# Out-projection of a short-convolution block: float32 sums in memory, spread residual loads, early operand work a step later, last tiles by token block

## The chip, the cores and the metric

The kernel runs on 1 core of one Trainium2 chip. The metric is the device time of one launch in microseconds (us). Engines are named as the profile names them: PE is TensorE (matmuls; PEld its weight loads), DVE is VectorE, ACT is ScalarE, POOL is GpSimd and SP is SyncE, which here only issues DMAs. POOL issues DMAs too, on a queue of its own.

## What is computed

With DEPTH = 1 only the first layer and the final norm remain of the reference:

```python
x = x + short_conv_mixer(rmsnorm(x, norm0_w), conv0_w_in, conv0_w_conv, conv0_w_out)
return rmsnorm(x, norm_f_w)

def short_conv_mixer(h, w_in, w_conv, w_out):
    b_gate, c_gate, u, z = jnp.split(h @ w_in, 4, axis=-1)
    cu = c_gate * u
    conv = causal depthwise convolution of cu, width 3
    y = b_gate * conv * jax.nn.silu(z)
    return y @ w_out
```

x has 1024 tokens of 2048 float32 values; w_in is 2048 x 8192, w_out 2048 x 2048.

## The kernel before

**Arithmetic.** Every float32 operand of a matmul is split into a rounded high part and the rest, a low part (`split`, lines 104 to 106: a copy on ACT, then a subtraction on DVE), and three matmuls (high x high, high x low, low x high, `PASSES`) make one product. Two-by-two blocks of each product are formed by seven sums of blocks instead of eight products (`PRODUCTS` 1, 5, 6, 2, 7, 3, 4); the sums of operands that this needs are made on DVE (`sub` line 109, `add` line 112).

**Order of the work.** All work is a list of steps, each with `loads`, `add`, `split`, `mm` and `evac`. The loop at the end emits, at step i, the loads, adds and splits of the steps ahead, then the matmuls of step i and what follows from them. `early` steps (i < 6) load one step ahead and split nothing ahead; later ones load 6 steps ahead, add 3 and split 2 ahead. Each engine takes its instructions strictly in the resulting order, so an instruction that waits holds up all behind it on its engine.

**Stages.** (1) `classical`, 8 steps, 384 matmuls: the first block of 128 channels, all four gates, plain products. Its operands need no token scale, so that x can be squared and summed meanwhile (`square`, in the `evac` of steps 0 to 3); the scale `rbc` comes from the sums through a power on POOL and two small DMAs (`token_scale`, lines 193 to 195). From step 4 on, `evac` also prepares the operands of all later blocks (class `XPrep`: load `xa`, `norm` line 137, then `item(r, j)` for each product). The 8 sums in PSUM are scaled out of it in step 7 (`g<-pc`, line 338). (2) `block`, 30 blocks of 7 steps of 24 matmuls, 5040 in all; the result y of 128 channels goes to `y_dram` (line 223, POOL queue) at the end of each block in the second half. The last block's y is made right after its last matmuls. (3) `out_block(db)`, twice 28 steps (7 products r by 4 pieces u) of 24 matmuls, 1344 in all. A step needs a sum of pieces of w_out (`wo`) and a sum of pieces of y. With db = 0 the y pieces are read from `y_dram` (`yr`, line 478, SP queue, 512 KB in rows of 2 KB), summed on DVE, split to high and low (`Y`, pool `xp`), used, and the split pair is stored to `s_dram` (`sd`, line 539, POOL queue, 1 MB); with db = 1 the pair is read back (line 502, POOL queue, 1 MB) and used as it is.

**Pools.** `xp` has 14 tiles of 8 KB per partition (operands X, then Y and the residual rows `st`), `t4` 16 of 4 KB (all raw loads, sums, gates), `wp` 3 (split weights), PSUM 8 banks.

**Ends.** `open_out` (lines 603 to 614), called one step ahead of the out-projection, loads all eight 1 MB residual tiles `st` and the weight `wf` of the final norm on the POOL queue. `evac` adds each finished sum to its residual; after the last product of a token block, `finish` (lines 616 to 634) forms the norm and stores the tile: sum of squares on ACT, a reduction and a scale on DVE, a power on POOL, a scaling shared by ACT and DVE, two stores. In the very last step (r = 4, u = 3, db = 1) the matmuls run token block by token block (`order`).

```python
for i, s in enumerate(steps):
    early = i < 6
    upto("load", i + (2 if early else LOAD_AHEAD + 1))
    ...
    if i == first_out - 1:
        open_out()
    upto("add", i + 1 if early else i + AHEAD + 2)
    upto("split", i + (1 if early else AHEAD + 1))
    s.mm()
    s.evac()
```

## Time and profile before

| | us |
|---|---|
| median of 3 runs (1603.18 to 1604.12) | 1603.95 |
| the profiled execution's own time | 1604.42 |
| its span in the profile | 1602.6 |
| PE busy (share of the span) | 1551.5 (97%) |
| DVE busy | 1030.0 (64%) |
| ACT busy | 508.6 (32%) |
| POOL busy | 106.2 (7%) |
| moved by DMA | 323.61 MB, mean 202 GB/s |
| chain that ended last: PE | 84% |
| chain that ended last: DMA | 8% |
| chain that ended last: DVE | 5% |

The span is what the profiler saw between the first and the last instruction; the 1.8 us between it and the execution's own time lie around it. Busy shares are means over the whole span, and the three stages have different limits, so the page's share says little about one of them: times are taken from the stretch in which they lie. A busy PE is not one at full speed, since its clock can be lowered (column PEclk, the granted clock: 1.00 is 2.4 GHz, 0.50 is 1.2 GHz).

### The profile page before, as it was taken

To read this page: it belongs to the slowest core of one execution; us is meant where nothing else is said; L and a number is where in the kernel's file an instruction comes from. 1 tells how busy PE (TensorE), PEld (TensorE's weight loads), DVE (VectorE), ACT (ScalarE), POOL (GpSimd) and SP (SyncE) were. 2 spreads that over 40 slices of the span, in tenths; PEclk is the share of its full clock that TensorE was granted. 3 is DMA by queue.
4 is the path that set the end of the run, shared out by engine and by line. 5 is a ranking of instruction groups with operands and counts; after the bars stand their busy time and mean duration, and the time that the engine had idled before them with its cause. 6 is when DMAs were issued, how large, how long until landed. Compare 5 with 4: busy or idle time off the path is not lost.

```text
span 1602.6 us, 17246 instructions
## 1 busy us (share of the span) xinstructions
PE 1551.5 (97%) x6777; PEld 1278.1 (80%) x6777; DVE 1030.0 (64%) x1116; ACT 508.6 (32%) x633; POOL 106.2 (7%) x200
## 2 busy tenths in 40 slices
PE   9899999999999999999999999999999797899996
PEld 7678888888888888888888888888888685788885
DVE  4598555554555544467777777777776785766344
ACT  7364333333333333222222222222222232441234
POOL 0000010100000100200000000000001110110001
PEclk9999999999999999999999999999999898999998
DMA  9715453443444443953344434334336999999755
GB/s 365 292 47 194 141 182 121 167 161 131 145 161 145 174 163 119 409 222 125 128 135 129 137 122 134 129 119 130 121 118 263 343 400 387 392 417 336 269 195 210
DMA packets 83953, 323.61 MB, mean 202 GB/s; under 512 B 8976, under 2 KB 9504, under 8 KB 73888
## 3 DMA queue, kind: packets, MB, share of 16 engines
q1 hardware_dynamic: 55872, 180.38, 33.1%
q0 software_dynamic: 26704, 137.93, 22.5%
q10 hardware_dynamic: 1296, 4.20, 0.7%
q8 instruction: 53, 0.87, 0.2%
q14 instruction: 28, 0.23, 0.0%
HBM read 230.20 MB, written 92.28 MB: 201 GB/s over the span
## 4 chain that ended last, share of the span: by engine, by line
PE 84%; DMA 8%; DVE 5%; issue 1%; ACT 1%; SPq 0%; POOL 0%; DVEq 0%; POOLq 0%; ACTq 0%
PE pa L415 40%; PE pc L415 20%; PE pb L415 10%; PE poa L549 7%; DMA yr<-y_dram 3%; PE poc L549 3%; PE pob L549 3%; DMA xsq<-in_x_dram 2%; DMA wo<-in_w_out_dram 2%; PE pc L301 1%; DVE wo L106 1%; DVE Y L106 1%; DVE yr L109 1%; DVE xa L137 1%; DVE wo L109 0%
## 5 line engine op out<-in xcount | busy, mean ns | idle before, releaser
L415 PE MATMUL pa<-X,w 128*128 128x512 f32 x2880 | 669.2, 390 | 9.4 <-DVE g L112 9.4
L415 PEld LDWEIGHTS pa<-X,w 128*128 128x128 f32 x2880 | 541.6, 188 | 122.2 <-DVE g L112 9.8
L415 PE MATMUL pc<-X,w 128*128 128x512 f32 x1440 | 336.1, 389 | 0.0
L415 PEld LDWEIGHTS pc<-X,w 128*128 128x128 f32 x1440 | 270.4, 188 | 56.0
L106 DVE TENSOR_TENSOR w<-wi,w 128x1024 fp32r<-128x1024 f32 x150 | 183.7, 1224 | 164.4 <-ACT w L105 163.5
L105 ACT CAST w<-wi 128x1024 fp32r<-128x1024 f32 x150 | 157.5, 1050 | 248.9 <-PE pa L415 189.9
L549 PE MATMUL poa<-wo,Y 128*128 128x512 f32 x768 | 178.6, 394 | 4.8 <-DVE wo L106 4.8
L549 PEld LDWEIGHTS poa<-wo,Y 128*128 128x128 f32 x768 | 146.1, 190 | 36.2 <-DVE wo L106 5.6
L415 PE MATMUL pb<-X,w 128*128 128x512 f32 x720 | 168.1, 389 | 0.0
L415 PEld LDWEIGHTS pb<-X,w 128*128 128x128 f32 x720 | 135.2, 188 | 28.0
L112 DVE TENSOR_TENSOR g<-pa,g 128x512 f32<-128x512 f32 x150 | 103.3, 689 | 74.1 <-PE pa L415 72.2
L105 ACT CAST w<-wt 128x1024 fp32r<-128x1024 f32 x60 | 63.4, 1056 | 247.2 <-PE pc L415 126.1
L549 PE MATMUL poc<-wo,Y 128*128 128x512 f32 x384 | 93.0, 403 | 11.6 <-DVE wo L106 9.3
L301 PE MATMUL pc<-xc,wc 128*128 128x512 f32 x384 | 90.6, 397 | 9.6 <-ACT xc L280 8.7
L106 DVE TENSOR_TENSOR wo<-wo,wo 128x1024 fp32r<-128x1024 f32 x56 | 68.4, 1222 | 47.5 <-ACT wo L105 47.4
L549 PEld LDWEIGHTS poc<-wo,Y 128*128 128x128 f32 x384 | 74.8, 196 | 29.1 <-DVE wo L106 10.0
L441 ACT COPY g<-pa 128x512 f32<-128x512 f32 x90 | 52.9, 588 | 139.1 <-PE pa L415 137.4
L301 PEld LDWEIGHTS pc<-xc,wc 128*128 128x128 f32 x384 | 72.7, 191 | 27.5 <-ACT xc L280 9.9
L105 ACT CAST wo<-wo 128x1024 fp32r<-128x1024 f32 x56 | 58.6, 1049 | 111.1 <-PE poa L549 48.2
L106 DVE TENSOR_TENSOR w<-wt,w 128x1024 fp32r<-128x1024 f32 x60 | 73.5, 1225 | 21.7 <-ACT w L105 21.5
L112 DVE TENSOR_TENSOR g<-pc,g 128x512 f32<-128x512 f32 x90 | 61.8, 687 | 37.8 <-PE pc L415 37.8
L109 DVE TENSOR_TENSOR wt<-wi,wi 128x1024 f32<-128x1024 f32 x60 | 73.4, 1223 | 3.0 <-DMA pd<-g 1.6
(83 smaller groups left out, 897.6 us busy)
## 6 DMA issues: line engine op xcount, KB each, us to landing
wi<-in_w_in_dram SPq DMA_DIRECT2D x120, 512.0 KB, 3.8
wo<-in_w_out_dram SPq DMA_DIRECT2D x64, 512.0 KB, 9.9
pd<-g POOLq DMA_DIRECT2D x60, 512.0 KB, 3.3
g<-pd SPq DMA_DIRECT2D x60, 512.0 KB, 4.7
sd<-Y POOLq DMA_DIRECT2D x28, 1024.0 KB, 8.6
Y<-sd POOLq DMA_DIRECT2D x28, 1024.0 KB, 6.6
yr<-y_dram SPq DMA_DIRECT2D x36, 512.0 KB, 10.8
xd<-xo POOLq DMA_DIRECT2D x28, 512.0 KB, 2.9
```

The source lines that it names most:

```text
L105: nc.scalar.copy(h, raw)
L106: nc.vector.tensor_tensor(l, raw, h.bitcast(F32), op=ALU.subtract)
L109: nc.vector.tensor_tensor(o, a, b, op=ALU.subtract)
L112: nc.vector.tensor_tensor(o, a, b, op=ALU.add)
L137: nc.vector.scalar_tensor_tensor(t, t, n0[:, k:k + 1], rbc, op0=ALU.mult, op1=ALU.mult)
L301: nc.tensor.matmul(state["ps"][2 * s + gi][h], wv[:, wz, gi, jj, s, :], xs[:, xz, h * NB:(h + 1) * NB], start=(a == 0 and jj == 0 and wz = ...
L415: nc.tensor.matmul(ps[where, s], wv[:, wz, j, s, :], xt[:, j % 2, xz, :], start=(r in (1, 5, 2) and j == 0 and wz == 0 and xz == 0), stop= ...
L441: nc.scalar.copy(o, ps[where, s])
L549: nc.tensor.matmul(ps[where, tb], Y[r, u][:, yz, jj * NB + tb * P:jj * NB + (tb + 1) * P], w["w"][:, wz, jj * NB:(jj + 1) * NB], start=(r ...
```

## The change

It has four parts.

1. **Stored sums.** For the products 5, 6, 3 and 7 the float32 sum of y pieces (512 KB) is stored to `s_dram` in the `add` of db = 0, and with db = 1 read back on the SP queue and split again. For the products 1, 2 and 4, which use a plain piece of y, nothing is stored, and db = 1 reads `y_dram` once more. So 28 stores and 28 loads of 1 MB become 16 stores of 512 KB on POOL and 28 loads of 512 KB on SP, and db = 1 gets 28 more splits.
2. **Spread residual loads.** The eight `st` tiles are loaded by twos at the steps -1, 0, 3 and 4 of the out-projection (`open_rows`), and `wf` at step 6, in one tile of `xp` instead of two of `t4`.
3. **First block.** Loading and splitting go one step further ahead from step 2 on (loads i + 3, splits i + 2); `norm` and the first items move from the `evac` of step 4 to that of step 5, half of step 5's to step 6; from step 6 on less is loaded, added and split ahead than before, until step 8.
4. **Last tiles.** The matmuls of (r = 4, db = 1) of u = 2 and u = 3 are emitted together, token block by token block, 12 matmuls each.

```diff
-    s_dram = {r: dram.tile([4, P, 2, 1024], F32R, name=f"sd_{r}") for r in PRODUCTS}
+    s_dram = {r: dram.tile([4, P, 1024], F32, name=f"sd_{r}") for r in (5, 6, 3, 7)}
...
                 if a == 4:
                     for j in range(4):
                         first_x.load(j, 0)
-                    for j in range(4):
-                        first_x.norm(j, 0)
-                    for j in range(4):
-                        first_x.item(1, j)
                 if a == 5:
                     for j in range(4):
                         first_x.load(j, 1)
                     for j in range(4):
+                        first_x.norm(j, 0)
+                        first_x.item(1, j)
+                    for j in range(2):
                         first_x.norm(j, 1)
-                    for j in range(4):
                         first_x.item(5, j)
                 if a == 6:
+                    for j in range(2, 4):
+                        first_x.norm(j, 1)
+                        first_x.item(5, j)
                     for r in (6, 2):
...
+                elif r in s_dram:
+                    w["y"] = {"s": f4(f"ys_{r}_{u}")}
+                    nc.sync.dma_start(w["y"]["s"], s_dram[r][u])
                 else:
-                    t = hl(xp, f"Y_{db}_{r}_{u}")
-                    nc.gpsimd.dma_start(t, s_dram[r][u])
-                    Y[r, u] = t
+                    n = {1: (0, 0), 2: (0, 1), 4: (1, 1)}[r]
+                    w["y"] = {n: yraw(n[0], n[1], u, f"{db}{r}{n[0]}{n[1]}")}
...
+                    if r in s_dram:
+                        nc.gpsimd.dma_start(s_dram[r][u], y[0, 0] if r == 7 else schain[u])
...
-                if db == 0:
...
+                if db == 1 and r in s_dram:
+                    src = y["s"]
+                else:
                     src = schain[u] if src is None else y[src]
-                    t = hl(xp, f"Y_{db}_{r}_{u}")
-                    split(src, t[:, 0, :], t[:, 1, :])
-                    nc.gpsimd.dma_start(s_dram[r][u], t)
-                    Y[r, u] = t
+                t = hl(xp, f"Y_{db}_{r}_{u}")
+                split(src, t[:, 0, :], t[:, 1, :])
+                Y[r, u] = t
...
+                if r == 4 and db == 1 and u >= 2:
+                    order = [(u, jj, tb) for tb in range(4) for u in (2, 3) for jj in range(2)] if u == 3 else []
...
+    def open_rows(th, tb):
+        t = xp.tile([P, D], F32, name=f"st_{th}_{tb}", tag="hl")
+        r0 = (th * 4 + tb) * P
+        nc.gpsimd.dma_start(t, x[r0:r0 + P, :])
...
+    def open_wf():
+        t = xp.tile([P, D], F32, name="wf", tag="hl")
...
     for i, s in enumerate(steps):
-        early = i < 6
-        upto("load", i + (2 if early else LOAD_AHEAD + 1))
+        early = i < 2
+        upto("load", i + (2 if early else 3 if i < 8 else LOAD_AHEAD + 1))
...
-        if i == first_out - 1:
-            open_out()
-        upto("add", i + 1 if early else i + AHEAD + 2)
-        upto("split", i + (1 if early else AHEAD + 1))
+        n = i - first_out
+        if n in (-1, 0, 3, 4):
+            for tb in range(2):
+                open_rows(n > 0, tb + 2 * (n in (0, 4)))
+        if n == 6:
+            open_wf()
+        upto("add", i + (1 if early else 2 if i < 8 else AHEAD + 2))
+        upto("split", i + (1 if early else 2 if i < 8 else AHEAD + 1))
```

**First place: VectorE ahead of the second step of the first block.** `w_1_5` is the split weight of that step (product 5), `wt_1` its sum, `X_r` the prepared operands of product r, `s` their sums. Before, `w_1_5` stands right behind X_2 and ahead of the eight `g` rows:

```order
L109 TENSOR_TENSOR s_1_682<-s_1_682,xa_582 128x512
L106 TENSOR_TENSOR X_6_0_777<-s_0_674,X_6_0_777 128x512
L109 TENSOR_TENSOR wi_1_00_697<-wi_1_11_701,wt_1_705 128x1024
L106 TENSOR_TENSOR X_6_1_784<-s_1_682,X_6_1_784 128x512 x2
L106 TENSOR_TENSOR X_2_0_790<-xa_662,X_2_0_790 128x512
L106 TENSOR_TENSOR X_2_0_790<-xa_664,X_2_0_790 128x512
L106 TENSOR_TENSOR X_2_1_795<-xa_666,X_2_1_795 128x512
L106 TENSOR_TENSOR X_2_1_795<-xa_668,X_2_1_795 128x512
L106 TENSOR_TENSOR w_1_5_801<-wt_1_705,w_1_5_801 128x1024
L338 TENSOR_TENSOR g_0_852<-pc_0_207,rbc 128x512
L338 TENSOR_TENSOR g_0_852<-pc_1_208,rbc 128x512
```

After, the same row stands behind the eight `g` rows, all of X_7 and half of X_3:

```order
L106 TENSOR_TENSOR X_7_1_859<-xa_593,X_7_1_859 128x512
L109 TENSOR_TENSOR xa_595<-xa_595 128x512
L109 TENSOR_TENSOR s_0_684<-xa_661,s_0_684 128x512
L109 TENSOR_TENSOR s_0_684<-xa_663,s_0_684 128x512
L106 TENSOR_TENSOR X_7_1_859<-xa_595,X_7_1_859 128x512
L106 TENSOR_TENSOR X_3_0_866<-s_0_684,X_3_0_866 128x512 x2
L109 TENSOR_TENSOR wt_1_876<-wi_1_01_786,wi_1_00_693 128x1024
L109 TENSOR_TENSOR s_1_753<-xa_665,s_1_753 128x512
L109 TENSOR_TENSOR wi_1_00_693<-wi_1_11_872,wt_1_876 128x1024
L106 TENSOR_TENSOR w_1_5_879<-wt_1_876,w_1_5_879 128x1024
L106 TENSOR_TENSOR X_3_1_918<-s_1_753,X_3_1_918 128x512
```

Counted from the first `norm` row to this split, VectorE has 44 rows' worth of work before (8 norms, 6 splits of `xc`, 6 full-width rows, 24 half-width rows) and 60 after (8, 2, 5 and 45): four of the six `xc` splits and one weight split went ahead of the norms, and 21 half-width rows, the eight `g` rows among them, came in.

**Second place: the POOL queue at the start of the out-projection.** `st` are the residual rows, `y_dram<-g` the results of the last two blocks, `sd` the stored operands. Before, all residual rows stand together:

```order
L608 DMA st_0_8111<-in_x_dram 128x2048
L539 DMA sd_164<-Y_1_0_8075 128x2048
L608 DMA st_1_8114<-in_x_dram 128x2048
L223 DMA y_dram<-g_3_7557 128x1024
L608 DMA st_2_8117<-in_x_dram 128x2048
L608 DMA st_3_8120<-in_x_dram 128x2048
L608 DMA st_0_8123<-in_x_dram 128x2048
L608 DMA st_1_8126<-in_x_dram 128x2048
L608 DMA st_2_8129<-in_x_dram 128x2048
L608 DMA st_3_8132<-in_x_dram 128x2048
L613 DMA wf_8135<-in_norm_f_w_dram 128x1024
L613 DMA wf_8137<-in_norm_f_w_dram 128x1024
```

After, four of the residual rows stand behind a stored sum `sd`, which VectorE makes, and the last block's y behind them:

```order
L612 DMA st_False_8110<-in_x_dram 128x2048
L223 DMA y_dram<-g_3_7554 128x1024
L612 DMA st_False_8160<-in_x_dram 128x2048
L612 DMA st_False_8163<-in_x_dram 128x2048
L530 DMA sd_164<-yr_0_8065 128x1024
L612 DMA st_True_8280<-in_x_dram 128x2048
L612 DMA st_True_8283<-in_x_dram 128x2048
L530 DMA sd_164<-yr_1_8103 128x1024
L530 DMA sd_164<-yr_2_8156 128x1024
L612 DMA st_True_8327<-in_x_dram 128x2048
L612 DMA st_True_8330<-in_x_dram 128x2048
L223 DMA y_dram<-g_3_7793 128x1024
```

So the second four can't be issued before VectorE has made the first sum; before, each waited for a free tile alone.

**Third place: VectorE at the very end.** `st<-poa` takes a finished sum out of PSUM, `tot` and the two rows behind it finish a tile. Before:

```order
L619 TENSOR_REDUCE tot_1_10251<-sums_1_8128 128x1
L112 TENSOR_TENSOR st_2_8129<-poa_2_9285,st_2_8129 128x512
L620 TENSOR_SCALAR tot_1_10251<-tot_1_10251 128x1
L112 TENSOR_TENSOR st_3_8132<-poa_3_9286,st_3_8132 128x512
L626 SCALAR_TENSOR_TENSOR st_1_8126<-st_1_8126,r_1_10254,wf_8135 128x512
L632 TENSOR_SCALAR st_1_8126<-st_1_8126,r_1_10254 128x512
L619 TENSOR_REDUCE tot_2_10263<-sums_2_8131 128x1
L620 TENSOR_SCALAR tot_2_10263<-tot_2_10263 128x1
L626 SCALAR_TENSOR_TENSOR st_2_8129<-st_2_8129,r_2_10266,wf_8135 128x512
L632 TENSOR_SCALAR st_2_8129<-st_2_8129,r_2_10266 128x512
L619 TENSOR_REDUCE tot_3_10275<-sums_3_8134 128x1
```

After, the third tile's row (`poa_2`) still stands ahead of the second tile's finishing, and the fourth tile's (`poa_3`) behind the third tile's finishing:

```order
L112 TENSOR_TENSOR st_True_8283<-poa_1_9276,st_True_8283 128x512
L624 TENSOR_REDUCE tot_1_10318<-sums_True_8285 128x1
L112 TENSOR_TENSOR st_True_8327<-poa_2_9277,st_True_8327 128x512
L625 TENSOR_SCALAR tot_1_10318<-tot_1_10318 128x1
L631 SCALAR_TENSOR_TENSOR st_True_8283<-st_True_8283,r_1_10321,wf 128x512
L637 TENSOR_SCALAR st_True_8283<-st_True_8283,r_1_10321 128x512
L624 TENSOR_REDUCE tot_2_10330<-sums_True_8329 128x1
L625 TENSOR_SCALAR tot_2_10330<-tot_2_10330 128x1
L631 SCALAR_TENSOR_TENSOR st_True_8327<-st_True_8327,r_2_10333,wf 128x512
L637 TENSOR_SCALAR st_True_8327<-st_True_8327,r_2_10333 128x512
L112 TENSOR_TENSOR st_True_8330<-poa_3_9278,st_True_8330 128x512
```

The fourth tile was taken out of PSUM ahead of the finishing of the second and third; now it comes behind both.

## Rows read from the trace of the kernel before

**Rows 1.** Busy time by stretch; matmuls in brackets, then clock, DMA share, GB/s.
```profile
0.00:61.10 61.10, 58.82 (x249) 45.99 (x249) 21.93 (x26) 37.09 (x51) 3.74 (x8) 1.00 0.99 379
61.10:104.80 43.70, 35.15 (x145) 28.11 (x145) 41.67 (x51) 20.95 (x29) 0.00 (x0) 0.92 0.32 108
104.80:1244.60 1139.80, 1139.80 (x5029) 943.82 (x5027) 742.50 (x787) 338.66 (x402) 67.12 (x126) 1.00 0.46 157
1244.60:1392.30 147.70, 121.91 (x494) 98.26 (x494) 109.47 (x108) 45.35 (x52) 14.37 (x27) 0.90 1.00 378
1392.30:1588.20 195.90, 195.86 (x865) 161.89 (x863) 108.97 (x134) 61.81 (x95) 19.37 (x36) 1.00 0.80 291
1588.20:1602.60 14.40, 0.00 (x0) 0.00 (x0) 5.42 (x15) 4.70 (x8) 1.62 (x3) 0.61 0.73 291
sum 1602.60, PE 1551.54 PEld 1278.07 DVE 1029.95 ACT 508.56 POOL 106.23; mean PE 258.59 PEld 213.01 DVE 171.66 ACT 84.76 POOL 17.71
```

**Rows 2.** The waits of TensorE, whole span.
```profile
PE pa L415 <- DVE g L112: 9.4, 1, 9.4
PE poc L549 <- DVE wo L106: 9.3, 2, 7.0
```

**Rows 3.** Timeline, 40 to 130 us: start, length, engine, line, operation, idle before.
```profile
55.98 0.55 POOL L195 DMA_DIRECT2D rbc<-rstd_dram  x1 [5.15 <-DMA rstd_dram<-rs]
...
63.13 3.68 DVE L137 SCALAR_TENSOR_TENSOR xa<-xa,n,rbc 128x1024 f32<-128x1024 f32 x3 [12.93 <-DMA rbc<-rstd_dram]
...
68.56 13.20 PE L301 MATMUL pc<-xc,wc 128*128 128x512 f32 x48 [7.42 <-ACT xc L280]
...
100.02 1.22 DVE L106 TENSOR_TENSOR w<-wt,w 128x1024 fp32r<-128x1024 f32 x1
...
110.25 5.60 PE L415 MATMUL pc<-X,w 128*128 128x512 f32 x24
```

**Rows 4.** Granted clock just after that wait, by two microseconds.
```profile
70.00:72.00 2.00, 2.00 (x5) 1.16 (x4) 2.00 (x3) 1.01 (x2) 0.00 (x0) 0.50 0.03 6
```

**Rows 5.** Timeline, the same stretch: VectorE rows that follow without a gap.
```profile
66.73 0.68 DVE L106 TENSOR_TENSOR X<-xa,X 128x512 fp32r<-128x512 f32 x1
...
91.13 1.22 DVE L109 TENSOR_TENSOR wt<-wi,wi 128x1024 f32<-128x1024 f32 x1
92.27 0.69 DVE L106 TENSOR_TENSOR X<-s,X 128x512 fp32r<-128x512 f32 x1
...
97.61 2.50 DVE L106 TENSOR_TENSOR X<-xa,X 128x512 fp32r<-128x512 f32 x4
```

**Rows 6.** Timeline of the SP queue, first 75 us.
```profile
33.63 4.17 SPq L183 DMA_DIRECT2D xsq<-in_x_dram  x4
```

**Rows 7.** Timeline, 1180 to 1300 us: the hand-over to the out-projection.
```profile
1222.52 0.53 POOL L223 DMA_DIRECT2D y_dram<-g  x1 [2.87 <-DVE g L222]
...
1231.81 0.38 SPq L478 DMA_DIRECT2D yr<-y_dram  x1
...
1232.75 0.94 SPq L478 DMA_DIRECT2D yr<-y_dram  x2
...
1252.14 1.22 DVE L112 TENSOR_TENSOR yr<-yr,yr 128x1024 f32<-128x1024 f32 x1 [17.64 <-DMA yr<-y_dram]
```

**Rows 8.** DMA issues, 1254 to 1392 us: KB each, us from issue to landing.
```profile
DMA packets 14624, 52.11 MB, mean 378 GB/s; under 512 B 1229, under 2 KB 1229, under 8 KB 11808
...
sd<-Y POOLq DMA_DIRECT2D x23, 1024.0 KB, 8.7
```

**Rows 9.** Timeline, 1560 us to the end.
```profile
1566.24 21.92 PE L549 MATMUL poa<-wo,Y 128*128 128x512 f32 x96
...
1575.41 1.22 DVE L106 TENSOR_TENSOR wo<-wo,wo 128x1024 fp32r<-128x1024 f32 x1
...
1593.45 0.58 ACT L585 ACTIVATE poa<-st 128x512 f32<-128x512 f32 x1
...
1596.37 0.37 ACTq L634 DMA_DIRECT2D out_dram<-st  x1
```

More of the change, by code (lines that the diff above doesn't have):

```diff
@@ L466, in out_block @@
     def out_block(db):
-        chain, schain, ps = {}, {}, {}
+        chain, schain, ps, wo = {}, {}, {}, {}
         ycols = (slice(0, NB), slice(NB, T))
@@ L532, in split_w @@
                 split(src, w["w"][:, 0, :], w["w"][:, 1, :])
-                if db == 0:
-                    y = w["y"]
-                    src = {1: (0, 0), 2: (0, 1), 4: (1, 1), 7: (0, 0)}.get(r)
+                y = w["y"]
+                src = {1: (0, 0), 2: (0, 1), 4: (1, 1), 7: (0, 0)}.get(r)
+                if db == 1 and r in s_dram:
+                    src = y["s"]
+                else:
                     src = schain[u] if src is None else y[src]
-                    t = hl(xp, f"Y_{db}_{r}_{u}")
-                    split(src, t[:, 0, :], t[:, 1, :])
-                    nc.gpsimd.dma_start(s_dram[r][u], t)
-                    Y[r, u] = t
+                t = hl(xp, f"Y_{db}_{r}_{u}")
+                split(src, t[:, 0, :], t[:, 1, :])
+                Y[r, u] = t
             def mm():
@@ L546, in mm @@
                         ps[where, tb] = bank(f"po{where}_{db}_{tb}")
-                for jj, tb in order(r, u):
+                wo[r, u] = w["w"]
+                if r == 4 and db == 1 and u >= 2:
+                    order = [(u, jj, tb) for tb in range(4) for u in (2, 3) for jj in range(2)] if u == 3 else []
+                else:
+                    order = [(u, jj, tb) for jj in range(2) for tb in range(4)]
+                for v, jj, tb in order:
                     for yz, wz in PASSES:
@@ L550, in mm @@
                             ps[where, tb],
-                            Y[r, u][:, yz, jj * NB + tb * P:jj * NB + (tb + 1) * P],
-                            w["w"][:, wz, jj * NB:(jj + 1) * NB],
-                            start=(r in (1, 5, 2) and u == 0 and jj == 0 and yz == 0 and wz == 0),
-                            stop=(r in (4, 3, 2) and u == 3 and jj == 1 and yz == 1),
+                            Y[r, v][:, yz, jj * NB + tb * P:jj * NB + (tb + 1) * P],
+                            wo[r, v][:, wz, jj * NB:(jj + 1) * NB],
+                            start=(r in (1, 5, 2) and v == 0 and jj == 0 and yz == 0 and wz == 0),
+                            stop=(r in (4, 3, 2) and v == 3 and jj == 1 and yz == 1),
                             skip_group_check=True,
                         )
-            def order(r, u):
-                if u == 3 and r == 4 and db == 1:
-                    return [(jj, tb) for tb in range(4) for jj in range(2)]
-                return [(jj, tb) for jj in range(2) for tb in range(4)]
             def evac():
@@ L601, in hybrid_kernel @@
     nc.vector.memset(pw1, -0.5)
-    def open_out():
-        for th in range(2):
-            for tb in range(4):
-                t = xp.tile([P, D], F32, name=f"st_{th}_{tb}", tag="hl")
-                r0 = (th * 4 + tb) * P
-                nc.gpsimd.dma_start(t, x[r0:r0 + P, :])
-                st[th, tb] = t
-                sums[th, tb] = const.tile([P, 4], F32, name=f"sums_{th}_{tb}")
-        for i in range(2):
-            t = f4(f"wf_{i}")
-            nc.gpsimd.dma_start(t, norm_f_w[i * 1024:(i + 1) * 1024].partition_broadcast(P))
-            wf.append(t)
+    def open_rows(th, tb):
+        t = xp.tile([P, D], F32, name=f"st_{th}_{tb}", tag="hl")
+        r0 = (th * 4 + tb) * P
+        nc.gpsimd.dma_start(t, x[r0:r0 + P, :])
+        st[th, tb] = t
+        sums[th, tb] = const.tile([P, 4], F32, name=f"sums_{th}_{tb}")
+    def open_wf():
+        t = xp.tile([P, D], F32, name="wf", tag="hl")
+        nc.gpsimd.dma_start(t, norm_f_w.partition_broadcast(P))
+        wf.extend([t[:, 0:1024], t[:, 1024:D]])
     def finish(th, tb, chunk):
```

## Prediction

> **What bounds the kernel now.** I read the busy time by stretch first, then the waits of TensorE, then the timeline around each wait. [Rows 1] cuts the span where TensorE's state changes. In the long stretch from 104.80 to 1244.60 us it never stops: 5029 recorded matmuls in 1139.80 us, 0.2266 us each. That is the price of a matmul at full clock. The stretch from 1392.30 to 1588.20 is full as well. Nothing can be won in these two but by fewer matmuls, and the change leaves their number alone. The loss lies in three places.
>
> First, 61.10 to 104.80: 145 matmuls cost 32.9 us and took 43.7, so 10.8 us are lost. [Rows 3] says why: the token scale `rbc` is asked for at 55.98 and VectorE can use it at 63.13; TensorE resumes at 68.56 after 7.42 us of waiting for an operand split that stood behind the `norm` rows. It resumes slowly: 48 matmuls take 13.20 us instead of 10.9, and [rows 4] shows the granted clock at 0.50. A long wait therefore costs its own length and 2.3 us more.
>
> Second, 1244.60 to 1392.30, the first five products of the out-projection: 494 matmuls cost 112.0 us and took 147.7, so 35.7 us are lost [rows 1]. DMA moves 378 GB/s at a share of 1.00 there: transfers are the limit. VectorE is busy for 109.5 us, nearly as long as the matmuls need, so it can't make up for a wait either. [Rows 2] has the single longest wait, 9.4 us.
>
> Third, the end: TensorE's last matmul ends at 1588.16 [rows 9], and 14.4 us follow [rows 1].
>
> **The first block.** A step further ahead in loading puts step 5's weights and x (1.5 MB, 1.57 million bytes) in front of the last four squares loads [rows 6] on the SP queue. The queue runs at 379 GB/s with a share of 0.99 up to 61.10 [rows 1], so the squares, the scale and `rbc` come 4.1 us later: VectorE starts its norms at 67.2 instead of 63.13. In exchange the splits of steps 5 and 6 no longer wait for them. TensorE then passes 61.10 without a stop, and the eight steps end at 94.0 (61.1 plus 32.9).
>
> From there on VectorE decides. [Rows 5] and [rows 3] give its pace in unbroken runs: 1.20 us for a full-width multiply (three from 63.13 to 66.73), 1.14 us for a full-width add or split (91.13 to 92.27), 0.60 us for a half-width one (four from 97.61 to 100.02). I check the pace on the kernel before: 14 x 1.20 + 6 x 1.14 + 24 x 0.60 = 38.0 us from 63.13 gives 101.2 for the split `w_1_5`; the trace ends it at 101.24 [rows 3]. After the change the same row comes behind 10 x 1.20 + 5 x 1.14 + 45 x 0.60 = 44.7 us, so at 111.9. Product 1 can start when the first two `g` rows have freed its banks: 12.0 + 2.3 + 15.6 = 29.9 us behind the scale, 97.1. It ends at 102.5, and product 5 waits from there to 111.9. That is 9.4 us, longer than the wait behind which the clock was halved, so 2.3 us more: in effect 114.2, where it began at 110.25 before [rows 3]. **This part costs 4.0 us.** From below: `rbc` no later and no clock loss, 107.8, a gain of 2.4. From above: `rbc` 2 us later still, a loss of 6. I take 4.0, since the queue was full in either case. Later splits are no problem: the next weights follow within 6 us, one per 5.4 us of TensorE.
>
> **The stored sums.** In the stretch of 147.7 us DMA moved 55.8 MB. Of these, 23 stores of the split pair (24.1 MB) go [rows 8]; about 14 stores of 0.52 MB come, and some 2 MB of residual rows that were early before: about 41 MB. At 378 GB/s they last 108 us, against 112 us of matmuls. So transfers no longer set the pace, but barely. Product 7 alone has four loads and a store per step, 2.6 MB or 6.9 us against 5.4 us: 6 us over its four steps if nothing was loaded ahead.
>
> The Trainium skill speaks against this part: "DMA: Bandwidth & Descriptors", section Bandwidth, asks for transfers of 1 MiB or more for 75% of peak, with 341 GB/s at 1 MB and 138 at 64 KB. The rows up to 61.10, whose loads are of 512 KB or less, reach 379 GB/s, so this trace doesn't agree. By the rule, at an estimated 240 GB/s halfway between, 41 MB would last 171 us and the sum below would come to 1629.
>
> In the second half each step splits its y again: 28 splits, 32 us on VectorE (1.14 each) and about as much on ScalarE. VectorE is busy for 109.0 of 195.9 us there and ScalarE for 61.8 [rows 1], so this costs nothing; were VectorE full, it would cost the 32 us. The 28 reloads move from POOL's queue to SP's; both run with spare share there (0.80), at half the bytes.
>
> **Spread residual rows.** Before, the pair of `yr` loads issued at 1232.75 reached VectorE only at 1252.14 [rows 7], and VectorE, which had waited 17.64 us, held back the two rows that free TensorE's banks: the 9.4 us of [rows 2]. Six of the eight residual rows stood on POOL's queue behind the y of 1222.52; the next `yr` load waited for that y until 1231.81. Now two stand there; the other four residual rows come behind a sum that VectorE makes. Four rows less are 4.2 MB, 11 us: the pair lands near 1241, ahead of the 1244.6 at which TensorE stopped. I cost this wait at nothing; the cover is some 4 us. What is late next is the last block's y, behind the second four rows on the same queue: 5.8 MB with the sums, 15 us, about as long as VectorE needs to make that y. `wf` in one tile of `xp` leaves two tiles of `t4` to the loads and five of `xp` to Y, of which three are in use: nothing.
>
> Between 0 (all hidden) and 15 us (product 7's 6 us and a second hand-over wait of 9.4) I leave **4 us of the 35.7** standing, nearest to product 7's figure with part of it loaded ahead. Gain 31.7.
>
> **The last tiles.** Token blocks now end 2.72 us apart (12 matmuls), and only the last remains after TensorE. Its operands are there: the split of u = 3 ends at 1576.6 [rows 9], 11.5 us before the end, and is used 9.5 us before it. From a tile's square to its store's issue pass 2.9 us (1593.45 to 1596.37), and the last issue is 8.2 us behind TensorE [rows 9]. Were the last tile alone, it would be 0.7 + 2.9 = 3.6. But its row stands behind the third tile's finishing, and the second's behind the third's sum, which ends 2.7 us before the end: A finishing holds VectorE for about 2.1 us (the 2.9 without the square's 0.8 on ScalarE): the second tile's from 2.1 to 0 us before the end, the third's for 2.1 behind it, so 2.1 + 3.6 = 5.7. **Gain 2.5 us**; between 0 and 4.6.
>
> **Sum.** 1604.4 (the profiled execution) + 4.0 - 31.7 - 2.5 = 1574.2 us. That execution stands 0.5 above the median of the runs, so 1573.7 against 1603.95.
>
> **The rivals.**
> (a) The hand-over wait survives: the pair or the last y lands late, VectorE has no spare time to recover, and 9 to 15 us more are lost: 1580 to 1588. For it: VectorE's 109.5 against 112 us, and the residual rows' share of a full queue. Against: 4.2 MB less ahead of the pair.
> (b) All goes better: `rbc` isn't late, the out-projection runs clean, the last tile follows at once: 1603.95 - 2.4 - 35.7 - 4.6 = 1561. Against: the count of VectorE rows, which fitted before to 0.1 us.
> (c) Slower: DMA keeps moving at a lower rate once its largest transfers are gone. With R in GB/s the stretch lasts 41,000 / R us; below 274 GB/s it takes as long as now and the kernel is slower by the first block's 4 us. The lowest row near it is 291, where the share is 0.80 [rows 1]. At 250, an assumed value below that row, 164 us: 1621. Against: 379 GB/s up to 61.10.
> The rule of the Trainium skill named above would be a cause of (c).
>
> **The numbers.** The forecast (1566 to 1580) 0.58, (a) 0.24, (b) 0.12, (c) 0.04, and 0.02 that the transfers' gain fails in part so that first block and gain cancel. About 0.2% (3.2 us) is what a measurement of this kernel can tell from no change; the forecast, (a) and (b) all lie beyond it: faster 0.94, same 0.02, slower 0.04. The range of 1562 to 1588 holds the forecast, all of (a) and the upper half of (b).
>
> **What would show it.** First block: the first norm near 67, TensorE waiting 8 to 11 us for `w` on line 106 near 102 to 112, and clock 0.50 behind it; no wait near 61. Without that wait, the first part is wrong. Out-projection: no wait of 9 us on a `g` row, 16 stores `sd` of 512 KB, DMA share just under 1.00 until product 7. Many waits of VectorE on `yr` would speak for (a). End: the last store issued 5 to 6 us behind the last matmul.

## The result

| | before | changed | ratio, 95% interval |
|---|---|---|---|
| median, us | 1603.57 (4 runs) | **1574.07** (1573.17 to 1577.51, 4 runs) | 0.9821 [0.9804, 0.9838] |
| profiled execution, its span | 1604.42, 1602.6 | 1573.39, 1571.6 | |

The forecast was 1573.7 with a range of 1562 to 1588. The total came out, but not by its terms: three of them were mis-sized, by -3.0, +3.5 and -1.3 us, and their errors cancel. That the sum came within 1 us is luck.

### The profile after

The busy time by stretch, with the columns of [rows 1] and its cuts up to 1392.30; the last cut is TensorE's new end.

```profile
61.10:104.80 43.70, 39.87 (x168) 32.19 (x166) 38.83 (x53) 15.93 (x25) 0.00 (x0) 0.96 0.25 96
104.80:1244.60 1139.80, 1135.48 (x5000) 939.78 (x5001) 746.26 (x786) 340.33 (x402) 66.04 (x124) 1.00 0.46 157
1244.60:1392.30 147.70, 143.45 (x618) 116.35 (x617) 125.10 (x128) 59.12 (x75) 10.12 (x19) 0.99 0.89 337
1392.30:1561.00 168.70, 168.67 (x745) 139.32 (x743) 118.95 (x141) 75.37 (x100) 3.25 (x6) 1.00 0.51 173
```

The gain is in the third of these lines: 618 matmuls in the 147.7 us that held 494 [rows 1]. The second has 29 fewer than before: the loss at the start has moved behind 104.8. The waits of TensorE over the whole span, for comparison with [rows 2]:

```profile
PE pc L416 <- ACT w L105: 6.2, 1, 6.2
PE poc L560 <- DVE wo L106: 3.1, 3, 1.9
PE pa L416 <- DVE g L339: 1.9, 1, 1.9
```

The first block, timeline from 55 to 122 us (start, length, engine, line, operation, idle before), to be read beside [rows 3]:

```profile
58.81 0.55 POOL L195 DMA_DIRECT2D rbc<-rstd_dram  x1 [4.75 <-DMA rstd_dram<-rs]
...
65.93 2.48 DVE L137 SCALAR_TENSOR_TENSOR xa<-xa,n,rbc 128x1024 f32<-128x1024 f32 x2 [9.79 <-DMA rbc<-rstd_dram]
...
95.59 7.32 PE L416 MATMUL pa<-X,w 128*128 128x512 f32 x24 [1.95 <-DVE g L339]
...
108.02 1.04 ACT L105 CAST w<-wt 128x1024 fp32r<-128x1024 f32 x1 [0.49 <-DVE wt L109]
...
109.12 7.76 PE L416 MATMUL pc<-X,w 128*128 128x512 f32 x24 [6.21 <-ACT w L105]
...
109.64 1.23 DVE L106 TENSOR_TENSOR w<-wt,w 128x1024 fp32r<-128x1024 f32 x1
...
116.72 5.60 PE L416 MATMUL pa<-X,w 128*128 128x512 f32 x24
```

The scale is 2.8 us later (58.81 against 55.98). TensorE passes 61 without a stop and stops twice later; each time 24 matmuls take over 7 us where 5.44 is the pace. The first of the two stops is hidden, since product 5 waits for its weights anyway. Product 6 begins at 116.72; before it began at 115.69 (5.44 behind the 110.25 of [rows 3]). **The first block costs 1.0 us between these two traces.** That holds to the end of the long stretch: the last product ahead of the out-projection begins at 1242.79; before it began at 1241.77 and would have ended at 1247.21 but for the wait of 9.4 us [rows 2].

The hand-over, 1239 to 1280 us, beside [rows 7]:

```profile
1239.45 3.41 SPq L479 DMA_DIRECT2D yr<-y_dram  x2
1241.25 1.23 DVE L112 TENSOR_TENSOR yr<-yr,yr 128x1024 f32<-128x1024 f32 x1 [1.23 <-DMA yr<-y_dram]
...
1248.24 26.21 SPq L479 DMA_DIRECT2D yr<-y_dram  x2
...
1271.14 0.54 POOL L223 DMA_DIRECT2D y_dram<-g  x1 [13.33 <-DVE g L222]
...
1278.05 1.23 DVE L112 TENSOR_TENSOR yr<-yr,yr 128x1024 f32<-128x1024 f32 x1 [3.21 <-DMA yr<-y_dram]
```

The pair reaches VectorE at 1241.25 instead of 1252.14, and TensorE's wait of 9.4 us is gone. But SP then stands from 1248.24 to 1274.45 at the first load that needs the last block's y, whose store is issued at 1271.14. What it waited for in that time, by the profile, and DMA's share (0.39) in the middle of it:

```profile
SPq L479 <- DMA y_dram<-g: 19.4, 1, 19.4
SPq L479 <- DMA yr<-y_dram: 6.0, 1, 6.0
```
```profile
1260.00:1272.00 12.00, 11.42 (x48) 8.85 (x48) 12.00 (x12) 5.40 (x6) 0.54 (x1) 1.00 0.39 160
```

So the first 6 us went to another load, and 19.4 to the last y. What follows is seen on TensorE, product by product (96 matmuls, 21.76 us at full pace):

```profile
1248.23 11.27 PE L560 MATMUL poa<-wo,Y 128*128 128x512 f32 x49
...
1271.70 11.51 PE L560 MATMUL poc<-wo,Y 128*128 128x512 f32 x49
...
1294.19 21.92 PE L560 MATMUL poa<-wo,Y 128*128 128x512 f32 x96
...
1317.27 5.76 PE L560 MATMUL poc<-wo,Y 128*128 128x512 f32 x24 [0.93 <-DVE wo L106]
1324.96 18.41 PE L560 MATMUL poc<-wo,Y 128*128 128x512 f32 x71 [1.94 <-DVE wo L106]
1343.21 21.92 PE L560 MATMUL poa<-wo,Y 128*128 128x512 f32 x96
1364.97 21.92 PE L560 MATMUL pob<-wo,Y 128*128 128x512 f32 x96
```

From start to start, products 1, 5, 6, 3 and 7 take 23.5, 22.5, 21.8, 27.3 and 21.8 us: 7.9 us lost, 5.5 of them in product 3, none in product 7. With 0.2 us in the rest, TensorE ends at 1560.97, 8.2 us behind 1248.23 plus 1344 matmuls of 0.2266. Before, the same sum from 1247.21 to 1588.16 left 36.4. **The out-projection gains 28.2 us.**

The end, from 1539 us, beside [rows 9]:

```profile
1539.73 21.24 PE L560 MATMUL poa<-wo,Y 128*128 128x512 f32 x93
...
1566.47 0.37 ACTq L639 DMA_DIRECT2D out_dram<-st_True  x1
```

The last store is issued 5.5 us behind TensorE's last matmul (8.2 before) and the span ends 5.1 us behind that (6.2 before). **The end gains 3.8 us.** Together 1.0 - 28.2 - 3.8 = -31.0, the difference of the spans.

### The profile page after: what moved, and what is told of

The parts are those of the page before. It is cut to its first block, busy times and chain, and to the rows that moved or that the text cites. A ratio compares the mean times of both kernels' runs of the same rounds, so it can differ in the third digit from the quotient of the medians.

```text
span 1571.6 us, 17261 instructions
## 1 busy us (share of the span) xinstructions
PE 1546.3 (98%) x6777; PEld 1274.0 (81%) x6777; DVE 1060.8 (68%) x1144; ACT 536.7 (34%) x661; POOL 84.2 (5%) x159
## 3 DMA queue, kind: packets, MB, share of 16 engines
q10 hardware_dynamic: 1296, 4.20, 0.7%
## 4 chain that ended last, share of the span: by engine, by line
PE 49%; issue 38%; DMA 7%; DVE 3%; POOL 1%; ACT 0%; SPq 0%; POOLq 0%; DVEq 0%; ACTq 0%
PE pa L416 20%; PE pc L416 10%; PE poa L560 8%; PE pb L416 5%; PE poc L560 3%; PE pob L560 3%; DMA xr<-in_x_t_dram 2%; DMA xsq<-in_x_dram 1%; DMA wo<-in_w_out_dram 1%; DVE X L106 1%; DMA X<-xd 1%; DMA yr<-y_dram 1%; DVE xa L137 1%; DMA sd<-yr 0%; POOL y_dram L223 0%
## 5 line engine op out<-in xcount | busy, mean ns | idle before, releaser
L105 ACT CAST wo<-wo 128x1024 fp32r<-128x1024 f32 x56 | 58.7, 1049 | 102.5 <-PE poa L560 39.2
L109 DVE TENSOR_TENSOR wt<-wi,wi 128x1024 f32<-128x1024 f32 x60 | 73.4, 1223 | 4.3 <-DMA pd<-g 2.8
```

What stands on the lines that cost most here:

```text
L105: nc.scalar.copy(h, raw)
L109: nc.vector.tensor_tensor(o, a, b, op=ALU.subtract)
```

## The experiments

All times are medians; kernels with the same time of before in the table shared their chip and its runs of before. The changed kernel itself, 0.9821 [0.9804, 0.9838], was timed beside other runs of before. Only no_sums, item7_first and combined have intervals that don't touch its interval. The other differences are a few us in size, and what is said of them rests on the traces, each of one execution.

| run | us | ratio to before | runs of before, us |
|---|---|---|---|
| no_first_block | 1573.01 | 0.9812 [0.9800, 0.9825] | 1602.97 |
| no_spread | 1578.59 | 0.9847 [0.9833, 0.9862] | 1602.97 |
| no_sums | 1600.30 | 0.9983 [0.9975, 0.9991] | 1602.97 |
| no_tail | 1577.47 | 0.9841 [0.9828, 0.9854] | 1602.97 |
| pool_yr | 1577.16 | 0.9837 [0.9824, 0.9851] | 1603.53 |
| item7_first | 1568.62 | 0.9783 [0.9770, 0.9796] | 1603.53 |
| items_later | 1570.34 | 0.9796 [0.9783, 0.9809] | 1603.53 |
| both | 1571.78 | 0.9801 [0.9788, 0.9814] | 1603.53 |
| y_late | 1576.46 | 0.9836 [0.9822, 0.9849] | 1602.72 |
| w5_first | 1570.26 | 0.9801 [0.9788, 0.9814] | 1602.72 |
| half_rows | 1570.48 | 0.9799 [0.9786, 0.9812] | 1604.42 |
| combined | 1567.38 | 0.9766 [0.9753, 0.9780] | 1603.83 |

### One part undone at a time

**The first block** as before (its calls of `norm` and `item`, and):

```
-        early = i < 2
+        early = i < 6
-        upto("load", i + (2 if early else 3 if i < 8 else LOAD_AHEAD + 1))
+        upto("load", i + (2 if early else LOAD_AHEAD + 1))
...
-        upto("add", i + (1 if early else 2 if i < 8 else AHEAD + 2))
-        upto("split", i + (1 if early else 2 if i < 8 else AHEAD + 1))
+        upto("add", i + (1 if early else AHEAD + 2))
+        upto("split", i + (1 if early else AHEAD + 1))
```

> The first block as before, the other three parts as in the change. Theory, from the two traces: the reordered first block costs 1.0 us (product 6 of the first channel block starts at 116.72 us instead of 115.69), so this kernel takes 1.0 us less than the changed one, about 1573. Rival, the prediction's own term: the part costs 4.0 us, so 1570. If it comes out above 1575, the part was a gain after all. In the trace the wait of about 7.4 us before a matmul near 61 us comes back and the 6.2 us one near 103 goes.

1573.01, as the theory gave, but not for its reason. In this trace the wait near 61 is back (8.56 us) and product 6 starts at 116.71, as in the changed kernel; `rbc` was asked for at 56.82, 0.8 us later than in the profile of before. The 1.0 us between the first two traces is thus no more than their scatter, and the 1.1 us between the medians lies inside the intervals. The part costs and gains nothing that shows.

**The spread rows:**

```
-        if n in (-1, 0, 3, 4):
-            for tb in range(2):
-                open_rows(n > 0, tb + 2 * (n in (0, 4)))
+        if n == -1:
+            for th in range(2):
+                for tb in range(4):
+                    open_rows(th, tb)
```

> All eight residual rows on POOL's queue at once, one step ahead of the out-projection; the rest as in the change. Theory: the four more rows (4.2 MB, 11 us at 378 GB/s) stand ahead of the pair of yr loads again, VectorE gets it near 1252 instead of 1241, and TensorE stops at the hand-over for 8 to 11 us on a row that frees its banks: 1580 to 1584. Rival A: the halved stores alone had made room, the rows are hidden anyway: 1573 to 1576. Rival B: with no second four rows ahead of the last y, SP's stop behind that y shortens and gives back what the hand-over costs: 1573 to 1577, but with the 8 us wait in the trace and no wait in product 3.

1578.59, 4.5 us more; the mechanism of the theory, at half its size. The load, VectorE's wait for it and TensorE's (a row of the timeline and two of the waits from 1230 us on):

```profile
1235.76 17.15 SPq L479 DMA_DIRECT2D yr<-y_dram  x2
```
```profile
DVE yr L112 <- DMA yr<-y_dram: 12.9, 1, 12.9
```
```profile
PE poa L560 <- DVE wo L106: 4.9, 1, 4.9
```

Behind that wait products 5 and 6 run at full pace (21.8 us each) and SP's stop at the last y is 10.4 us long, so rival B has a share too; but product 3 still loses 4.9 us, which rival B had at nothing.

**The stored sums:** the pair is split, stored and reloaded as before.

```
+                    t = hl(xp, f"Y_{db}_{r}_{u}")
+                    nc.gpsimd.dma_start(t, s_dram[r][u])
...
+                    nc.gpsimd.dma_start(s_dram[r][u], t)
```

> The high/low pairs stored (28 stores of 1 MB) and reloaded as before, instead of 16 stores of the float32 sums; the rest as in the change. Theory: bytes set the pace of the first five products: some 17 MB more at 378 GB/s are 45 us of transfer, of which about 15 us fit into the spare share that the stretch has now, so the kernel takes 25 to 30 us more: 1595 to 1604. Rival: the wait at the hand-over was the larger part and spreading the rows removed it; then at most 10 us more: below 1585.

1600.30: 26.2 us more, the theory's case. This is the part that the gain rests on. The same stretch as in [rows 1], and TensorE's waits:

```profile
1244.60:1392.30 147.70, 127.64 (x523) 102.74 (x522) 112.69 (x114) 50.90 (x62) 14.92 (x28) 0.93 1.01 393
```
```profile
PE poc L555 <- DVE wo L106: 7.7, 3, 3.9
PE poa L555 <- DVE wo L106: 7.5, 2, 7.1
PE pa L416 <- DVE g L112: 4.8, 1, 4.8
```

DMA is full again (1.01, 393 GB/s), with 523 matmuls instead of 618, although the rows are spread. The run changes the number, the size and the queue of the transfers together; that the bytes are what counts rests on that full DMA.

**The order of the last product:**

```
-                if r == 4 and db == 1 and u >= 2:
-                    order = [(u, jj, tb) for tb in range(4) for u in (2, 3) for jj in range(2)] if u == 3 else []
+                if r == 4 and db == 1 and u == 3:
+                    order = [(u, jj, tb) for tb in range(4) for jj in range(2)]
```

> The last product's matmuls in the order of before (block by block only within the last quarter, 1.36 us apart), the rest as in the change. Theory: what follows TensorE's last matmul grows by the 3.8 us that the two traces show (10.6 to 14.4): 1577.9. Rival, the prediction's term: 2.5 us, 1576.6; the rest of the 3.8 would then come from stores that land sooner because DMA is freer, and stay.

1577.47, 3.4 us more. TensorE's end and the last issue in this trace:

```profile
1540.46 21.92 PE L560 MATMUL poa<-wo,Y 128*128 128x512 f32 x96
```
```profile
1570.59 0.37 ACTq L639 DMA_DIRECT2D out_dram<-st_True  x1
```

TensorE ends at 1562.38 and the last store is issued 8.2 us later, as before the change; it lands 5.3 us after that (span 1575.9). So the order is worth 2.7 us (8.2 to 5.5); the faster landing stays without it. The rest of the 3.4 is TensorE's end, 1.4 us later in this execution.

The four differences add up to -1.1 + 4.5 + 26.2 + 3.4 = 33.0 us, against 29.5 for the whole change. The 3.5 us between can be the scatter of five medians, or the parts depend on each other: without the stored sums, the other three together are worth 2.7 us (1602.97 to 1600.30), where one at a time they were worth 6.8.

### What the first block waits for

**item7_first** makes the operands of product 7 ahead of the `g` rows and those of product 2 behind them; **items_later** (the second diff) makes both behind them, as background work of which it does three pieces per step instead of two up to step 15. Each asks for product 5's add and split in step 7.

```
-                    for r in (6, 2):
+                    for r in (6, 7):
...
+                    upto("add", 10)
+                    upto("split", 10)
                     for j in range(4):
-                        first_x.item(7, j)
+                        first_x.item(2, j)
```
```
-                    for r in (6, 2):
-                        for j in range(4):
-                            first_x.item(r, j)
+                    for j in range(4):
+                        first_x.item(6, j)
...
+                    upto("add", 10)
+                    upto("split", 10)
+                    for r in (2, 7, 3, 4):
+                        for j in range(4):
+                            background.append(lambda j=j, r=r: first_x.item(r, j))
...
-        for _ in range(2):
+        for _ in range(3 if i < 16 else 2):
```

> The changed kernel, with the operands of product 7 made ahead of those of product 2 (in front of the g rows) and product 5's add and split asked for right behind the g rows. Theory: product 5 waits because its weights come late: they wait for a t4 buffer that an x tile of product 7 holds until about 102 us; with these tiles freed by 94 the weights land before 98, product 1 starts near 98 (2.4 us later, four more wide rows' worth less four half ones) and product 5 near 104.5 instead of 109.1: product 6 starts at 110 to 112 instead of 116.7, 1568 to 1570. Rival, the prediction's count of VectorE rows alone: the rows ahead of the split for product 5 are four half ones fewer and none of the rest is late, so 2.4 us less: 1571.5. Third: any saved wait is lost again at product 2, whose operands are late now: 1574.

> The changed kernel, with the operands of products 2 and 7 both made behind the g rows, and product 5's add and split asked for ahead of them. Theory (the t4 buffer): the x tiles of product 7 are freed no sooner than now, so the weights for product 5 land near 106 as now; product 1 starts 2 us earlier and waits are only longer behind it: 1573 to 1575. Rival (VectorE's order): the add and the split for product 5 stand ahead of 16 half-width rows, so product 5 follows product 1 at once: about 6 us less, 1568.

Both are faster than the changed kernel, 1568.62 and 1570.34. item7_first's time is the one that its theory gave, but the theory of the buffer falls by the other run: items_later leaves the x tiles as late as they are (the next weights are asked for at 103.88 instead of 102.07) and still gains 3.7 us. It doesn't reach its rival's 1568 either, since product 5's add began only at 103.77, behind half-width rows that it should have stood ahead of, and product 5 at 106.19. The timeline of SP in the changed kernel had already spoken against the buffer:

```profile
59.65 0.98 SPq L362 DMA_DIRECT2D wi<-in_w_in_dram  x2
...
102.07 0.93 SPq L362 DMA_DIRECT2D wi<-in_w_in_dram  x2
```

The two tiles of which product 5's weights are made were loaded at 59.65; it is the third and fourth, for products 6 and 2, that wait for a buffer until 102. Product 5 waits for its place in VectorE's order. **w5_first** puts that add and split ahead:

```
+                    upto("add", 10)
+                    upto("split", 10)
                     g = [f4(f"g_{c}_{i}") for i in range(4)]
...
+                    for r in (7, 2):
+                        for j in range(4):
+                            first_x.item(r, j)
```

> The changed kernel, with product 5's add and split ahead of the last g rows, and the operands of products 7 and 2 behind them. Theory (VectorE's order of rows alone sets product 5, its weights lie there from about 65 us): product 1 starts by 95 us without a wait over 1 us and product 5 follows at once near 100 instead of 109.1. Product 6 then waits: its second weight tile gets its buffer only when the operands of product 7 are split (about 101), and VectorE reaches its row near 108: product 6 at 109 to 111.5 instead of 116.7, so 5 to 7 us less than the changed kernel, 1567 to 1569. Rival (the buffer holds product 5 as well): product 5 not before 105, product 6 at 112 to 113: 1570.

```profile
94.94 5.69 PE L418 MATMUL pa<-X,w 128*128 128x512 f32 x24 [1.12 <-DVE g L340]
...
100.47 5.60 PE L418 MATMUL pc<-X,w 128*128 128x512 f32 x24
...
108.54 1.22 DVE L109 TENSOR_TENSOR wi<-wi,wt 128x1024 f32<-128x1024 f32 x1
...
110.89 0.88 PE L418 MATMUL pa<-X,w 128*128 128x512 f32 x2 [4.83 <-ACT w L105]
```

Product 5 follows product 1 at 100.47, 8.65 us earlier than in the changed kernel, and product 6 waits instead. VectorE's order is shown for product 5. It holds product 6 too: the weight that was late for its buffer is asked for at 102.04, the loads there land 4.0 us behind their issue (median of two), and VectorE, which is busy for all of the time from 94 to 111, comes to product 6's sum only at 108.54. The time, 1570.26, is 1.3 us above the theory's range: behind the wait of 4.83 us the granted clock was 0.66 from 111 to 116, and the 48 matmuls from 110.89 on took 12.8 us instead of 10.9. The out-projection starts at 1244.36 here and at 1243.44 in item7_first (1248.23 in the changed kernel).

### What is left in the out-projection

**pool_yr:** two loads of `y` go to POOL's queue.

```
-            nc.sync.dma_start(t.rearrange("p (j t) -> p j t", j=2), yv[half, :, u, :, ycols[th]])
+            q = nc.gpsimd if name == f"5{th}{half}" and u == 3 else nc.sync
+            q.dma_start(t.rearrange("p (j t) -> p j t", j=2), yv[half, :, u, :, ycols[th]])
```

> The changed kernel, with the two yr loads of the fourth step of product 5 (one of them is the first that needs the last block's y) issued by POOL instead of SP. Theory: what is left in the out-projection is SP standing for 26 us behind that y (1248.24 to 1274.45) with DMA at a share of 0.39, so that the loads for product 3 come late and it loses 5.5 us in waits and clock (27.3 us for 96 matmuls instead of 21.8); with SP free that goes: about 5 us less, 1569, and no wait of TensorE between 1300 and 1345. Rival, the prediction: it is the bytes of product 7 that leave about 4 us standing; then the order of the queues changes nothing, 1573 to 1575.

1577.16, 3.1 us more: neither. In the profiled execution the out-projection begins at 1249.94, 1.7 us later than in the changed kernel, and product 2 at 1368.04, 3.1 us later. Its timeline:

```profile
1280.30 0.72 POOL L480 DMA_DIRECT2D yr<-y_dram  x1 [7.07 <-DMA y_dram<-g]
...
1286.23 1.22 DVE L112 TENSOR_TENSOR yr<-yr,yr 128x1024 f32<-128x1024 f32 x1 [6.89 <-DMA yr<-y_dram]
...
1288.64 12.56 PE L561 MATMUL poc<-wo,Y 128*128 128x512 f32 x47 [3.83 <-DVE wo L106]
```

Other loads of SP now move while the last y is stored: it lands 7.3 us behind its issue instead of 2.9, is read back more slowly too, and reaches VectorE at 1286.23 instead of 1278.05. The wait moves to product 5, which loses 6.0 us, while product 3 loses 1.7 instead of 5.5. SP's stop had kept the way clear for the very store that it waited for. SP wasn't wholly free, either: it stood 10.2 us for a row of VectorE (L109) and, behind its issue of 1272.43, 7.1 us for the same store.

**both** has the edits of pool_yr and item7_first.

> The changed kernel with the edits of the two runs above, pool_yr and item7_first. They touch places 1100 us apart, so both gains should add: about 10 us less than the changed kernel, 1563 to 1565. If one theory falls, only the other's 5 us: 1568 to 1570.

1571.78: item7_first's gain and pool_yr's loss, added.

**y_late**, on the list of (product, step) of the first half:

```
+        if db == 0:
+            todo.insert(10, todo.pop(7))
```

> The changed kernel; in the first half of the out-projection the fourth step of product 5 (the first that needs the last block's y) goes behind the third step of product 6, three steps later on every engine. Theory: what is left of the loss is the way of that y (VectorE makes it by 1270.8, it is stored, lands, is read back by 1278): SP stands for it and VectorE too. With its use 16 us later SP stands for about 10 us instead of 26, VectorE doesn't wait for the last yr, the loads for product 3 come in time: of the 8.1 us lost behind 1248 about 5 go: 1568 to 1570, and product 3's 96 matmuls take under 24 us instead of 27.3. Rival, from the run with POOL's queue: whatever lets SP go on only makes the store of the last y land later (7.1 us instead of 3.3) and the wait moves to product 5 or 6: 1573 to 1577. Second rival, the prediction: product 7's bytes leave the loss standing, 1573 to 1575.

1576.46. In this kernel product 6's fourth weight is subtracted into the running sum ahead of product 5's fourth split, so that product 5 computes with another operand there and also waits for loads that it doesn't need. That alone can make waits, so the time decides nothing on the theory. SP's stop fell from 26.2 to 8.8 us all the same, and DMA stood at 1.00 from 1248 to 1296.

**half_rows** takes bytes away instead:

```
-        nc.gpsimd.dma_start(t, x[r0:r0 + P, :])
+        load_half(th, tb, 0)
...
+        if b:
+            nc.gpsimd.tensor_copy(t[:, 0, 1, 0:1], sums[th, tb][:, 2:3])
+        nc.gpsimd.dma_start(t[:, :, b, :], r[:, :, b, :])
...
+        if n in (26, 30):
+            for tb in range(4):
+                load_half(n == 30, tb, 1)
```

> The changed kernel; of each residual row tile only the two quarters that the first half of the out-projection adds to are loaded where the whole tile was (0.5 instead of 1 MB), the other two are loaded behind product 3 and product 7 (an eight-times tiny copy on POOL keeps them there). Theory, from the run that let SP go on and gained nothing while DMA stood at a share of 1.00 up to 1296: it is the bytes between the hand-over and product 7 that set the time, not the order of the queues. 4.2 MB less there are 11 us at 378 GB/s: most of the 8.1 us lost behind 1248 goes, 1566 to 1569, and product 3's wait with it. Rival: the way of the last y (stored, landed, read back; SP and VectorE stand for it) sets it, which these bytes don't shorten by more than 2 to 3 us: 1571 to 1574.

1570.48, 3.6 us less, between the two, and with a range that overlaps the changed kernel's (1569.90 to 1574.12). TensorE by product, and one stretch of its busy time:

```profile
1248.36 21.92 PE L560 MATMUL poa<-wo,Y 128*128 128x512 f32 x96
1270.12 21.92 PE L560 MATMUL poc<-wo,Y 128*128 128x512 f32 x96
1291.88 21.92 PE L560 MATMUL poa<-wo,Y 128*128 128x512 f32 x96
...
1361.49 21.92 PE L560 MATMUL pob<-wo,Y 128*128 128x512 f32 x96
```
```profile
1260.00:1272.00 12.00, 12.00 (x55) 9.93 (x54) 10.41 (x10) 3.06 (x3) 0.56 (x1) 1.00 0.21 68
```

Products 1, 5 and 6 lose nothing now; 4.3 us remain in 3 and 7 (from 1248.36 to 1361.49 are 113.1 us, five products cost 108.8). SP still stands for 24 us, and DMA is at 0.21 meanwhile. The last y is stored 4.4 us sooner (issued at 1266.70), so the bytes and the way of that y were not taken apart.

**combined** has the edits of item7_first and half_rows, and `todo.insert(9, todo.pop(7))`.

> The changed kernel with three edits: item7_first, half_rows, and the fourth step of product 5 (with the last block's y) two steps later, behind the second step of product 6. From the runs before: item7_first alone gave 5.4 us and half_rows 3.6, at places far apart, so without the third edit 1565. Theory for the third: with 4 MB fewer the 4.3 us still lost behind 1248 come from SP standing 24 us for that y, with DMA at 0.21 of its share meanwhile; used 11 us later SP stands for 8 to 13 us and most of the 4.3 go: 1561 to 1563. Rival: as in the runs pool_yr and y_late, letting SP go on only makes the last y land later and the wait moves: 1565 to 1568.

1567.38, the lowest median of all (1.2 us under item7_first, with intervals that overlap), but by the rival for the third edit: the out-projection starts at 1243.39, product 2 at 1359.26, so 7.1 us are lost where half_rows lost 4.3. The wait is now at product 6:

```profile
1301.48 13.79 PE L562 MATMUL poa<-wo,Y 128*128 128x512 f32 x47 [3.26 <-DVE wo L106]
```

So 3.6 of the 7.9 us went with the 4.2 MB. The rest could not be moved away by either way of letting SP go on. item7_first and half_rows without the third edit, 1565 by their sum, were not run together; which resource holds the last 4 us stays open. No run moved VectorE's work on the last y: in the changed kernel the out-projection begins at 1248.23 and VectorE ends that y at 1270.84, with a wait of 4.74 us for a load and rows for the out-projection in between.

## Why the prediction came out

**The first block, +4.0: too much.** The count of VectorE's rows held: 44.7 us were forecast from the first norm to the end of the split `w_1_5`, and it took 44.9 (65.93 to 110.87). Two other steps failed. `rbc` came 2.8 us later, not 4.1. And "product 5 waits from there to 111.9" took the end of the split for its start: TensorE began at 109.12, behind the cast of the high part, while VectorE still made the low part. The half clock behind the wait was right: the granted clock was 0.50 from 108 to 112, and 24 matmuls in 7.76 us are 2.3 more than 5.44. The wait of 1.95 us before product 1, with its lower clock, was not foreseen, but cost nothing: in no_spread it was 0.57 us, product 1 took 5.72 us instead of 7.32, and product 6 began at 116.89 all the same. In sum +1.0 by the two traces, nothing by no_first_block.

**The out-projection, 4 us left standing: too little, and at another place.** 8.2 are left. The term was put down to product 7, "four loads and a store per step"; product 7 lost nothing. Product 3 lost 5.5, behind SP's stop. The prediction had named the last y as "late next" and held it to be covered, "about as long as VectorE needs to make that y"; the row that it didn't count is SP's: loads that need no y stand behind it for 26 us. That this stop costs the 5.5 is argued and not shown: product 3 loses 4.9 in no_spread with a stop of 10.4 us, and 2.7 in half_rows with one of 24.0. The two large steps held. The stored sums were the bulk of it (26.2 us in no_sums, which puts DMA back at 1.01 and 393 GB/s), and the pair of `yr` loads reached VectorE at 1241.25 where 1241 was forecast. The 28 splits of the second half cost nothing, as forecast: from 1392.30 to 1561.00 TensorE is busy for 168.67 of 168.70 us, with VectorE at 118.95.

**The last tiles, 2.5: right in its mechanism.** The last issue came 5.5 us behind the last matmul, against 5.7 forecast, and no_tail gives 2.7 us to the order. The other 1.1 us is that the store lands sooner, and no_tail has it as well; the prediction didn't look at it.

**Rival (c)** fell: with loads and stores of 512 KB, DMA moved 399 GB/s from 1296 to 1320 and 406 from 1320 to 1344.

```profile
1296.00:1320.00 24.00, 23.07 (x102) 18.78 (x101) 19.65 (x20) 10.21 (x10) 2.65 (x5) 1.00 1.03 399
1320.00:1344.00 24.00, 21.95 (x89) 17.34 (x88) 21.26 (x21) 7.35 (x7) 2.12 (x4) 0.93 1.04 406
```

The rule of the Trainium skill ("DMA: Bandwidth & Descriptors", section Bandwidth) that asks for 1 MiB or more, and by which 1629 was worked out, doesn't agree with this trace either.

Three figures of the rivals are slips that change nothing: in (c) 41 MB in 147.7 us are 278 GB/s and not 274, and its own sum, 1603.95 + 4.0 - 2.5 + 16.3, gives 1622 and not 1621; in (a) 9 to 15 us on top of 1573.7 are 1583 to 1589, not 1580 to 1588.

## What to carry to other kernels

Where DMA is at a share of 1.00 over a stretch, look for what is stored only to be read back: 23.1 MB instead of 58.7 (28 stores and 28 loads of 1 MB before) gave 26 of the 29.5 us, at the price of splits on engines that had room. When a wait goes, follow the queue that stood in it, too: an in-order queue that stops at one late transfer holds back all that need nothing late, but freeing it can slow the transfer that it waited for, as it did here. And for an in-order engine that is full, count its rows up to the one that another engine waits for; then look at which half of the operand the other engine really needs first.

## What was not expected of the hardware

- The same 512-KB store took 2.9 us from issue to landing with SP stopped and 7.3 us with loads of SP beside it. It took 7.2 us in the run both and 7.0 in y_late, where SP had issued loads just ahead of it too, and 2.9 in half_rows, where SP had stopped. The DMA issues of the two stretches (KB each, us to landing), of the changed kernel and of pool_yr:

```profile
y_dram<-g POOLq DMA_DIRECT2D x1, 512.0 KB, 2.9
```
```profile
y_dram<-g POOLq DMA_DIRECT2D x1, 512.0 KB, 7.3
```

- A wait of 1.95 us was followed by a granted clock of 0.56 (0.50 is 1.2 GHz), and the 24 matmuls behind it took 1.9 us more than at 2.4 GHz; in w5_first one of 1.12 us at the same place left them at 5.69 us. The changed kernel just behind the longer wait (its busy time by two microseconds):

```profile
96.00:98.00 2.00, 2.00 (x7) 1.56 (x6) 2.00 (x5) 0.00 (x0) 0.00 (x0) 0.56 0.00 0
```
